# RG-LRU gates as two 64-row products side by side in the TensorE array, in two PSUM banks

## The chip, the cores and the metric

The kernel runs on one core of one Trainium2 chip. The metric is the device time of one execution in microseconds (us). Before the change the median of 3 runs is 1001.49 us (998.43 to 1003.96). TensorE multiplies a stationary operand (loaded by LDWEIGHTS) with a moving operand and writes to PSUM, of which this kernel uses banks as tiles of 128x512 fp32. VectorE (DVE), ScalarE (ACT) and GpSimd (POOL) work beside it; SyncE (SP) and POOL issue DMAs.

## The reference

One step of a decoder layer on 1024 prompt tokens and 8 decode tokens. One input projection (1024 to 7176 columns) feeds an RG-LRU branch and an mLSTM branch; both are merged and projected back. The part that the change touches is the pair of gates of the RG-LRU branch: the 1024 channels are 16 blocks of 64, and each block has its own 64x64 weights for r and for i.

```python
blocks = xc.reshape(B, S, NB_A, BW_A)            # NB_A = 16 blocks of BW_A = 64
r = sigmoid(einsum('bsnc,ncd->bsnd', blocks, w_r).reshape(B, S, W_A) + b_r)
i = sigmoid(einsum('bsnc,ncd->bsnd', blocks, w_i).reshape(B, S, W_A) + b_i)
log_a = -LRU_C * r * softplus(-lam)
a = exp(log_a)
u = sqrt(-expm1(2.0 * log_a)) * (i * xc)         # h_t = a_t h_{t-1} + u_t
```

`xc` is the branch's input after a causal convolution of width 4. The 8 decode tokens go through the same gates with their own states.

## The kernel before

Channels lie on partitions, tokens along the free dimension. Products in full precision are made from three products of float32r halves: `split` (L70 on ScalarE, L71 on VectorE) gives a high and a low part, and `mm3` (L64 to L66) multiplies high by high, high by low and low by high into one bank.

The program has an opening (normalisation, first unit), then 13 more units of the input projection, two groups of 256 columns each, every unit cut into seven products of two halves (a Strassen scheme), then the mLSTM chunks with the output projection between them. The units run from about 85 us to 660 us. `pop_bg` hands out other work between the halves of the products: gate tables, the RG-LRU queue `rgq`, the decode queue. Instructions are queued per engine, each engine works through its queue in order, and a scheduler sets the final order of each queue, so a gate's products can stand between two products of a unit.

The RG-LRU branch is worked off in 16 halves: 8 groups `j` of 128 channels (two blocks of 64) by 2 halves of 512 tokens. A half has seven steps (`rg_half`): two of convolution, `gate_r`, `gate_i`, `decay`, `scan`, `outs`. For a group the raw gate weights are put in a 128x(2x128) tile `graw`, the two blocks of r on the diagonal of one 128x128 square, those of i on that of the other; the rest was set to zero once (L639). `ghi` and `glo` are its split. A gate is then one full 128-row `mm3` into the one bank of the tag "s", read by one ScalarE tanh (L729 for r, L735 for i). Since there is one "s" bank, the products of i wait for ScalarE's reading of r. After the second half of a group, `rg_dec` does the gates of the decode tokens the same way in plain fp32, two matmuls of 8 columns (L772), each shown as two passes, with tanh in L774.

The bank of the tag "tr" serves the decode tokens of the input projection: `dec_unit` (L229, 8 matmuls with 32 stationary columns, in four groups of columns of the array) writes it once per unit, ScalarE copies it out (L232), four transposes write it again (L237), and VectorE reduces that (L240).

Of the kernel before, what the change touches and what calls it, by code (L numbers as in the profile page):

```python
# [9 lines left out]
F32 = mybir.dt.float32  # L10
F32R = mybir.dt.float32r
BF16 = mybir.dt.bfloat16
AF = mybir.ActivationFunctionType
ALU = mybir.AluOpType
# [3 lines left out]
P = 128  # L18
T = 1024
HT = 512  # L20
NB = 8
# [8 lines left out]
R_CW, R_CB, R_BR, R_BI, R_LAM, R_GM, R_H0, R_CONV, R_N0, R_END = 0, 4, 5, 6, 7, 8, 9, 17, 41, 49  # L30
# [19 lines left out]
def hymba_kernel(  # L50
# [7 lines left out]
    V, A, G, TE = nc.vector, nc.scalar, nc.gpsimd, nc.tensor  # L58
    ld = nc.sync.dma_start
    stq = nc.gpsimd.dma_start  # L60

    def mm3(out, ah, al, bh, bl, first, last):

        TE.matmul(out, ah, bh, start=first, stop=False, skip_group_check=True)  # L64
        TE.matmul(out, ah, bl, start=False, stop=False, skip_group_check=True)  # L65
        TE.matmul(out, al, bh, start=False, stop=last, skip_group_check=True)  # L66
# [12 lines left out]
    def ps(tag, shape):  # L79
        return psp.tile(shape, F32, tag=tag, name=f"ps_{tag}", bufs=NBUF.get(tag, 1))  # L80

    def const(shape, name, dt=F32):
        return cpool.tile(shape, dt, tag=name, name=name)
# [14 lines left out]
    def sg(shape, name, dt=F32):  # L98

        return stg.tile(shape, dt, tag="stg", name=name)  # L100
# [4 lines left out]
    def dconst(shape, name):  # L105

        return dpool.tile(shape, F32, tag=name, name=name)
# [10 lines left out]
    PT = dconst([P, KC, R_END], "PT")  # L118
# [5 lines left out]
    hb = const([P, KC, 2], "hb")  # L124
# [12 lines left out]
    dgr = dconst([P, 2, KC, NB], "dgr")  # L137
# [219 lines left out]
    fp = es_f.enter_context(tc.tile_pool(name="f_start", bufs=1))  # L357
# [159 lines left out]
    fp = es_f.enter_context(tc.tile_pool(name="f_gates", bufs=1, reuse_waits="tile"))  # L517

    def gates():
# [24 lines left out]
        fx, ab, lg, z, z2, p = (gx[:, n, :] for n in range(6))  # L544
# [7 lines left out]
        lfd = lg[:, 32:64].rearrange("p (b h) -> p b h", h=NH)  # L552
        V.tensor_scalar(sp2, lg[:, 64:72], -2.0, None, op0=ALU.mult)
        V.tensor_scalar(sp4n, lg[:, 64:72], 4.0, None, op0=ALU.mult)
        V.tensor_scalar(hb, PT[:, :, R_BR:R_BR + 2], 0.5, None, op0=ALU.mult)
        V.tensor_scalar(gm4, PT[:, :, R_GM], 0.25, None, op0=ALU.mult)

        dgm = fp.tile([P, 2, NB, NH], F32, tag="dgm", name="dgm")
# [48 lines left out]
        for half in range(2):  # L607
            pk = ps(("s", "qp")[half], [P, 4, P])
            for q in range(4):
                c = half * 4 + q  # L610
                TE.transpose(pk[:, q, :], stk[:, c * P:(c + 1) * P], idF)
            s = slice(half * 4, half * 4 + 4)
# [17 lines left out]
    fpr = {}  # L630

    def rd_open():

        es_f.close()
        fpr["es"] = ExitStack()
        fpr["p"] = fpr["es"].enter_context(tc.tile_pool(name="f_rd", bufs=1, reuse_waits="tile"))
        fpr["graw"] = [fpr["p"].tile([P, 2, P], F32, tag=f"graw{i}", name=f"graw{i}") for i in range(2)]
        for t in fpr["graw"]:
            G.memset(t, 0.0)  # L639
        rg_gw(0)  # L640
        stq(s_conv[0, :, 0:2, :], st_conv[0, :, 1:3, :])
        dec_open()
# [4 lines left out]
    def rg_load(n, both=False):  # L647

        if n >= len(halves) or halves[n][0] not in rst["stored"]:
            return  # L650
        j, b = halves[n]
        if ("x", n) not in rst:
            xs = fpr["p"].tile([P, 3 + HT], F32, tag="xs", name="xs", bufs=2)
            if b == 0:
                V.memset(xs[:, 0:3], 0.0)
                ld(xs[:, 3:3 + HT], d_x[j][:, 0:HT])
            else:
                ld(xs, d_x[j][:, HT - 3:T])
            rst["x", n] = xs
        if both and ("z", n) not in rst:  # L660
            rst["z", n] = zs = fpr["p"].tile([P, HT], F32, tag="zsr", name="zsr", bufs=2)
            ld(zs, d_y[j][:, b * HT:(b + 1) * HT])
# [17 lines left out]
    def rg_gw(j):  # L680
        if j < KC:
            graw = fpr["graw"][j % 2]
            for n, src in enumerate((w_rgate, w_igate)):
                for two in range(2):
                    s = slice(two * 64, two * 64 + 64)
                    ld(graw[s, n, s], src[0, 2 * j + two])

    def rg_half(j, b):
        fp = fpr["p"]
        pc = lambda r, n=1: PT[:, j, r:r + n]  # L690
        st = {}

        n = 2 * j + b

        def conv1():
            rg_load(n, True)
            xs = st["xs"] = rst["x", n]
            rg_load(n + 1)
            if b == 0:
                rg_gw(j + 1)  # L700
                ghi = fp.tile([P, 2, P], F32R, tag="ghi", name="ghi")
                glo = fp.tile([P, 2, P], F32R, tag="glo", name="glo")
                split(ghi, glo, fpr["graw"][j % 2])
                rst["g", j] = ghi, glo
            st["xc"] = xc = fp.tile([P, HT], F32, tag="xc", name="xc")
            V.tensor_scalar(xc, xs[:, 3:3 + HT], pc(R_CW + 3), pc(R_CB), op0=ALU.mult, op1=ALU.add)
            for t in (2, 1):
                V.scalar_tensor_tensor(xc, xs[:, t:t + HT], pc(R_CW + t), xc, op0=ALU.mult, op1=ALU.add)

        def conv2():  # L710
            xs, xc = st["xs"], st["xc"]
            V.scalar_tensor_tensor(xc, xs[:, 0:HT], pc(R_CW), xc, op0=ALU.mult, op1=ALU.add)
            st["xh"] = fp.tile([P, HT], F32R, tag="xh", name="xh")
            st["xl"] = fp.tile([P, HT], F32R, tag="xl", name="xl")
            split(st["xh"], st["xl"], xc)
            if b == 1:
                V.tensor_copy(OC[:, j, 1:4], xs[:, HT:HT + 3])

        def gate(g):
            ghi, glo = rst["g", j]  # L720
            pg = ps("s", [P, 512])
            mm3(pg, ghi[:, g, :], glo[:, g, :], st["xh"], st["xl"], True, True)
            return pg

        def gate_r():
            rg_load(n + 1, True)
            pg = gate(0)
            st["rg"] = fp.tile([P, HT], F32, tag="rg", name="rg")
            A.activation(st["rg"], pg, AF.Tanh, scale=0.5, bias=hb[:, j, 0:1])  # L729

        def gate_i():
            pg = gate(1)

            st["na"], st["ig"] = (fp.tile([P, HT], F32, tag=t, name=m) for m, t in (("na", "xh"), ("ig", "xl")))
            A.activation(st["ig"], pg, AF.Tanh, scale=0.5, bias=hb[:, j, 1:2])  # L735
            A.activation(st["na"], st["rg"], AF.Tanh, scale=sp2[:, j:j + 1], bias=sp2[:, j:j + 1])
            A.activation(st["rg"], st["rg"], AF.Exp, scale=sp4n[:, j:j + 1], bias=sp4n[:, j:j + 1])
            V.scalar_tensor_tensor(st["ig"], st["ig"], 1.0, st["xc"], op0=ALU.add, op1=ALU.mult)

        def decay():  # L740
            rg, na = st["rg"], st["na"]
            V.scalar_tensor_tensor(na, rg, 1.0, na, op0=ALU.add, op1=ALU.mult)
            V.tensor_scalar(rg, na, -1.0, 1.0, op0=ALU.mult, op1=ALU.add)
            V.scalar_tensor_tensor(na, na, 2.0, na, op0=ALU.subtract, op1=ALU.mult)
            A.activation(na, na, AF.Sqrt, scale=-0.25)

        def scan():
            rg, ig, na = st["rg"], st["ig"], st["na"]
            V.tensor_tensor(ig, ig, na, op=ALU.mult)
            V.tensor_tensor_scan(na, rg, ig, 0.0 if b == 0 else OC[:, j, 0:1], op0=ALU.mult, op1=ALU.add)  # L750
            V.tensor_copy(OC[:, j, 0:1], na[:, HT - 1:HT])

        def outs():
            na, zs = st["na"], rst["z", n]
            V.scalar_tensor_tensor(na, na, 0.5, zs, op0=ALU.mult, op1=ALU.mult)
            mh, ml = sg([P, HT], "rmh", F32R), sg([P, HT], "rml", F32R)
            split(mh, ml, na)
            stq(d_rm[0, j, :, b * HT:(b + 1) * HT], mh.bitcast(F32))
            stq(d_rm[1, j, :, b * HT:(b + 1) * HT], ml.bitcast(F32))
        return [conv1, conv2, gate_r, gate_i, decay, scan, outs]  # L760

    def rg_dec(j):

        pc = lambda r, n=1: PT[:, j, r:r + n]
        xc = dxc[:, j, :]
        cst = PT[:, j, R_CONV:R_CONV + 24].rearrange("p (b t) -> p b t", t=3)
        V.tensor_scalar(xc, dxz[:, 0, j, :], pc(R_CW + 3), pc(R_CB), op0=ALU.mult, op1=ALU.add)
        for t in range(3):
            V.scalar_tensor_tensor(xc, cst[:, :, t], pc(R_CW + t), xc, op0=ALU.mult, op1=ALU.add)
        pg = ps("s", [P, 2, NB])  # L770
        for g in range(2):
            TE.matmul(pg[:, g, :], fpr["graw"][j % 2][:, g, :], xc, start=g == 0, stop=True, skip_group_check=True)  # L772
        for g in range(2):
            A.activation(dgr[:, g, j, :], pg[:, g, :], AF.Tanh, scale=0.5, bias=hb[:, j, g:g + 1])  # L774

    def rg_final():

# [609 lines left out]
    for n in range(4, N):  # L1387
        c, h = n // 4, n % 4
# [83 lines left out]
```

## Time and profile before

| What | Value |
|---|---|
| runs | 998.43, 1001.49, 1003.96 us |
| profiled execution | 1000.53 us, its span 998.8 us, mean granted clock 0.993 |
| TensorE busy | 959.2 us (96% of the span), 5756 matmul passes |
| VectorE, ScalarE, GpSimd busy | 704.7, 531.7, 149.7 us |
| gate products (L64 to L66 into ps_s from xh, xl) | 96, between 147.5 and 539.9 us |
| ScalarE reads of gates (L729, L735) | 32 of 687 ns |

TensorE is pipelined: the time of a matmul in a row runs until its end in PSUM and overlaps the next one. How fast they follow one another is read from the starts.

### The profile page before, as it was taken

What the parts mean: (1) busy time and instruction counts of PE and PEld (TensorE: products, weight loads), DVE (VectorE), ACT (ScalarE), POOL (GpSimd) and SP (SyncE); (2) the same over time, 40 slices, a digit from 0 to 9 for tenths busy, and PEclk for the clock granted to TensorE, in tenths of its full rate; (3) what the DMA queues carried; (4) which work ended last, traced back from release to release, by engine and by line L of the source; (5) the groups of instructions that cost most, each with busy time, mean ns of one, the idle gap of its engine ahead of it and who ended that gap; (6) DMA issues with size and microseconds to landing.
All of it is one profiled execution on the core that took longest, in us unless ns stands there. A gap on an engine that the chain in (4) does not pass through costs nothing. (4 is left out here: it accounts for less than half of the span.)

```text
span 998.8 us, 16047 instructions
## 1 busy us (share of the span) xinstructions
PE 959.2 (96%) x5756; PEld 792.2 (79%) x5756; DVE 704.7 (71%) x1478; ACT 531.7 (53%) x950; POOL 149.7 (15%) x259
## 2 busy tenths in 40 slices
PE   8999999999999999999999999999989989899996
PEld 7887767777787988777798999987668778778776
DVE  5776798988888878767877557676556746656754
ACT  5563436675765665635667544545345535535532
POOL 1111112121212122212213110102001000000111
PEclk9999999999999999999999999999999999999999
DMA  4441357356545647266536362337746245255431
GB/s 147 143 129 42 127 141 247 129 182 202 199 152 190 189 162 225 82 217 228 193 106 212 99 195 91 117 126 250 225 141 187 86 139 165 82 155 177 107 76 55
DMA packets 125465, 152.72 MB, mean 153 GB/s; under 512 B 14119, under 2 KB 104263, under 8 KB 125376
## 3 DMA queue, kind: packets, MB, share of 16 engines
q1 hardware_dynamic: 107656, 95.81, 32.4%
q0 software_dynamic: 17728, 55.87, 15.8%
q8 instruction: 45, 0.74, 0.3%
q14 instruction: 36, 0.29, 0.1%
HBM read 100.07 MB, written 51.65 MB: 152 GB/s over the span
## 5 line engine op out<-in xcount | busy, mean ns | idle before, releaser
L71 DVE TENSOR_TENSOR wl<-raw,wh 128x1024 fp32r<-128x1024 f32 x91 | 110.9, 1219 | 32.8 <-ACT wh L70 20.4
L70 ACT CAST wh<-raw 128x1024 fp32r<-128x1024 f32 x91 | 95.4, 1049 | 69.8 <-PE ps_o L65 21.8
L64 PE MATMUL ps_kv<-cb_hi,wh 128*128 128x512 f32 x256 | 102.5, 401 | 0.4 <-ACT s L310 0.4
L65 PE MATMUL ps_kv<-cb_lo,wh 128*128 128x512 f32 x256 | 100.2, 392 | 0.0
L66 PE MATMUL ps_kv<-cb_hi,wl 128*128 128x512 f32 x256 | 100.2, 391 | 0.0
L64 PE MATMUL ps_kv<-wh,cb_hi 128*128 128x256 f32 x320 | 91.9, 287 | 0.0
L66 PE MATMUL ps_kv<-wh,cb_lo 128*128 128x256 f32 x320 | 90.7, 283 | 0.0
L65 PE MATMUL ps_kv<-wl,cb_hi 128*128 128x256 f32 x320 | 90.7, 283 | 0.0
L64 PE MATMUL ps_o<-cb_hi,wh 128*128 128x512 f32 x192 | 75.6, 394 | 0.1
L66 PE MATMUL ps_o<-cb_hi,wl 128*128 128x512 f32 x192 | 74.9, 390 | 0.0
L65 PE MATMUL ps_o<-cb_lo,wh 128*128 128x512 f32 x192 | 74.9, 390 | 0.0
L64 PE MATMUL ps_o<-wh,cb_hi 128*128 128x256 f32 x240 | 68.8, 287 | 0.0
L66 PE MATMUL ps_o<-wh,cb_lo 128*128 128x256 f32 x240 | 68.0, 283 | 0.0
L65 PE MATMUL ps_o<-wl,cb_hi 128*128 128x256 f32 x240 | 68.0, 283 | 0.0
L64 PEld LDWEIGHTS ps_kv<-wh,cb_hi 128*128 128x128 f32 x320 | 61.2, 191 | 6.5 <-issue 3.4
L64 PEld LDWEIGHTS ps_kv<-cb_hi,wh 128*128 128x128 f32 x256 | 48.1, 188 | 19.5 <-issue 5.1
L1034 DVE SCALAR_TENSOR_TENSOR W<-W,be_t,maskT 128x128 f32<-128x128 f32 x32 | 11.2, 351 | 73.6 <-DMA W<-d_alpha 73.6
L66 PEld LDWEIGHTS ps_kv<-wh,cb_lo 128*128 128x128 f32 x320 | 61.3, 191 | 1.7 <-issue 1.7
L65 PEld LDWEIGHTS ps_kv<-wl,cb_hi 128*128 128x128 f32 x320 | 61.3, 192 | 1.0 <-issue 0.8
L66 PEld LDWEIGHTS ps_kv<-cb_hi,wl 128*128 128x128 f32 x256 | 48.0, 188 | 10.4
L65 PEld LDWEIGHTS ps_kv<-cb_lo,wh 128*128 128x128 f32 x256 | 48.1, 188 | 9.4
L64 PE MATMUL ps_o<-wo,mh 128*128 128x512 f32 (+1 forms) x136 | 53.6, 394 | 0.7 <-ACT mh L70 0.7
(465 smaller groups left out, 2651.0 us busy)
## 6 DMA issues: line engine op xcount, KB each, us to landing
raw<-in_w_in_dram SPq DMA_DIRECT2D x56, 512.0 KB
Cb<-in_state_mlstm_C_dram SPq DMA_DIRECT2D x32, 256.0 KB
out_dram<-Cb POOLq DMA_DIRECT2D x32, 256.0 KB, 4.5
qk<-d_qk SPq DMA_DIRECT2D x32, 256.0 KB
oraw<-in_w_out_dram SPq DMA_DIRECT2D x16, 512.0 KB
d_qk<-s POOLq DMA_DIRECT2D x24, 256.0 KB, 4.5
x<-in_x_prompt_dram SPq DMA_DIRECT2D x8, 512.0 KB
d_x<-s POOLq DMA_DIRECT2D x16, 256.0 KB, 2.7
```

Of the source, the lines that this page charges most:

```text
L64: TE.matmul(out, ah, bh, start=first, stop=False, skip_group_check=True)
L65: TE.matmul(out, ah, bl, start=False, stop=False, skip_group_check=True)
L66: TE.matmul(out, al, bh, start=False, stop=last, skip_group_check=True)
L70: A.copy(hi, src)
L71: V.tensor_tensor(lo, src, hi.bitcast(F32), op=ALU.subtract)
L1034: V.scalar_tensor_tensor(W, W, be_t[:, c, h:h + 1], maskT, op0=ALU.add, op1=ALU.min)
```

## The change

Each half now takes both gates in one step, `gate`. The two blocks of a group lie in rows 0 to 63 and 64 to 127 of the array. `graw` is 128x128: in rows 0 to 63 the r weights of the first block stand in columns 0 to 63 and its i weights in columns 64 to 127; in rows 64 to 127 the second block's i weights stand first, and its r weights in columns 64 to 127. So one 64-row product gives r and i of a block. Products of the lower rows go to the "s" bank, products of the upper rows to the "tr" bank, in turn: three pairs, six matmuls of 64 rows by 128 columns with 512 moving columns, where there were six of 128 by 128. There are no zero quarters left, and the two memsets are gone.

The reading is now four activations on 64 partitions: r from rows 0 to 63 of "s" and rows 64 to 127 of "tr", and i from the other half of each, written to the partitions of its channels (`gate_out`). The bias table `hb` has its i column swapped to fit, by three small VectorE operations in place of one. The two ScalarE functions of r and the first VectorE operation on i move to a step `gate2`, so that a half has seven steps as before. `rg_dec` does the same with two 64-row fp32 matmuls of 8 columns, one in each bank, and four activations of 64x8.

```diff
-        fpr["graw"] = [fpr["p"].tile([P, 2, P], F32, tag=f"graw{i}", name=f"graw{i}") for i in range(2)]
-        for t in fpr["graw"]:
-            G.memset(t, 0.0)
+        fpr["graw"] = [fpr["p"].tile([P, P], F32, tag=f"graw{i}", name=f"graw{i}") for i in range(2)]
...
-                    s = slice(two * 64, two * 64 + 64)
-                    ld(graw[s, n, s], src[0, 2 * j + two])
+                    c = (n + two) % 2 * 64
+                    ld(graw[two * 64:two * 64 + 64, c:c + 64], src[0, 2 * j + two])
+    LOHI = slice(0, 64), slice(64, 128)
+    def gate_out(rg, ig, pg, j):
+        for n in range(2):
+            A.activation(rg[LOHI[n]], pg[n][LOHI[n]], AF.Tanh, scale=0.5, bias=hb[LOHI[n], j, 0:1])
+        for n in range(2):
+            A.activation(ig[LOHI[n]], pg[n][LOHI[1 - n]], AF.Tanh, scale=0.5, bias=hb[LOHI[1 - n], j, 1:2])
...
-                ghi = fp.tile([P, 2, P], F32R, tag="ghi", name="ghi")
-                glo = fp.tile([P, 2, P], F32R, tag="glo", name="glo")
+                ghi = fp.tile([P, P], F32R, tag="ghi", name="ghi")
+                glo = fp.tile([P, P], F32R, tag="glo", name="glo")
...
-        def gate(g):
+        def gate():
+            rg_load(n + 1, True)
             ghi, glo = rst["g", j]
-            pg = ps("s", [P, 512])
-            mm3(pg, ghi[:, g, :], glo[:, g, :], st["xh"], st["xl"], True, True)
-            return pg
-        def gate_r():
-            rg_load(n + 1, True)
-            pg = gate(0)
+            pg = [ps(tag, [P, 512]) for tag in ("s", "tr")]
+            for k, (w, x) in enumerate(((ghi, st["xh"]), (ghi, st["xl"]), (glo, st["xh"]))):
+                for s, o in zip(LOHI, pg):
+                    TE.matmul(o, w[s, :], x[s, :], start=k == 0, stop=k == 2)
             st["rg"] = fp.tile([P, HT], F32, tag="rg", name="rg")
-            A.activation(st["rg"], pg, AF.Tanh, scale=0.5, bias=hb[:, j, 0:1])
-        def gate_i():
-            pg = gate(1)
             st["na"], st["ig"] = ...
-            A.activation(st["ig"], pg, AF.Tanh, scale=0.5, bias=hb[:, j, 1:2])
+            gate_out(st["rg"], st["ig"], pg, j)
+        def gate2():
             A.activation(st["na"], st["rg"], AF.Tanh, ...)
...
-        return [conv1, conv2, gate_r, gate_i, decay, scan, outs]
+        return [conv1, conv2, gate, gate2, decay, scan, outs]
...
-        pg = ps("s", [P, 2, NB])
-        for g in range(2):
-            TE.matmul(pg[:, g, :], fpr["graw"][j % 2][:, g, :], xc, start=g == 0, stop=True, skip_group_check=True)
-        for g in range(2):
-            A.activation(dgr[:, g, j, :], pg[:, g, :], AF.Tanh, scale=0.5, bias=hb[:, j, g:g + 1])
+        pg = [ps(tag, [P, NB]) for tag in ("s", "tr")]
+        for s, o in zip(LOHI, pg):
+            TE.matmul(o, fpr["graw"][j % 2][s, :], xc[s, :], start=True, stop=True)
+        gate_out(dgr[:, 0, j, :], dgr[:, 1, j, :], pg, j)
```

The order of the instructions moves with it. In the rows below the names are tiles: `wh`, `wl` the halves of a unit's weights, `cb_hi`, `cb_lo` the normalised input, `ps_s`, `ps_tr`, `ps_kv`, `ps_o` the PSUM tags; the last figure is the size of the output. Line numbers after L554 are higher in the changed kernel: the gate's products are L736, the decode gates' L779, the activations L694 (r) and L696 (i).

TensorE at the first half of the first group, before: the end of the r gate and, five products later, the i gate.

```order
L65 MATMUL ps_kv<-cb_lo_167,wh_3_1556 128x512
L66 MATMUL ps_kv<-cb_hi_166,wl_3_1557 128x512
L65 MATMUL ps_s<-xl,ghi 128x512
L66 MATMUL ps_s<-xh,glo 128x512
L64 MATMUL ps_kv<-cb_hi_166,wh_3_1556 128x512
L65 MATMUL ps_kv<-cb_lo_167,wh_3_1556 128x512
L66 MATMUL ps_kv<-cb_hi_166,wl_3_1557 128x512
L64 MATMUL ps_kv<-cb_hi_166,wh_3_1556 128x512
L65 MATMUL ps_kv<-cb_lo_167,wh_3_1556 128x512
L64 MATMUL ps_s<-xh,ghi 128x512
L65 MATMUL ps_s<-xl,ghi 128x512
L66 MATMUL ps_s<-xh,glo 128x512
```

The same place after the change, with both gates:

```order
L64 MATMUL ps_o<-cb_hi_164,wh_2_1485 128x512
L736 MATMUL ps_s<-xh,ghi 128x512
L736 MATMUL ps_tr<-xh,ghi 128x512
L65 MATMUL ps_o<-cb_lo_165,wh_2_1485 128x512
L66 MATMUL ps_o<-cb_hi_164,wl_2_1486 128x512
L64 MATMUL ps_kv<-cb_hi_166,wh_3_1556 128x512
L736 MATMUL ps_s<-xl,ghi 128x512
L736 MATMUL ps_tr<-xl,ghi 128x512
L736 MATMUL ps_s<-xh,glo 128x512
L736 MATMUL ps_tr<-xh,glo 128x512
L65 MATMUL ps_kv<-cb_lo_167,wh_3_1556 128x512
```

The pairs stand next to each other everywhere. In 5 of the 16 halves full-array products of the unit come between the first pair and the other two, as here; in the other 11 the six stand in one run. That makes 21 stretches of 64-row products.

TensorE at the first decode gate, before, and after. The product of the upper rows waits for VectorE's reading of the transposes (L237) in "tr", and the scheduler has put eight products of the unit before it.

```order
L237 MATMUL ps_tr<-idF,Z 128x128 x4
L772 MATMUL ps_s<-dxc,graw_1342 128x8 x2
L64 MATMUL ps_kv<-cb_hi_160,wh_0_1745 128x512
L65 MATMUL ps_kv<-cb_lo_161,wh_0_1745 128x512
L66 MATMUL ps_kv<-cb_hi_160,wl_0_1746 128x512
```

```order
L237 MATMUL ps_tr<-idF,Z 128x128 x4
L779 MATMUL ps_s<-dxc,graw_1344 128x8
L64 MATMUL ps_kv<-cb_hi_160,wh_0_1747 128x512
L65 MATMUL ps_kv<-cb_lo_161,wh_0_1747 128x512
L66 MATMUL ps_kv<-cb_hi_160,wl_0_1748 128x512
L64 MATMUL ps_kv<-cb_hi_160,wh_0_1747 128x512
L65 MATMUL ps_kv<-cb_lo_161,wh_0_1747 128x512
L66 MATMUL ps_kv<-cb_hi_160,wl_0_1748 128x512
L64 MATMUL ps_kv<-cb_hi_160,wh_0_1747 128x512
L65 MATMUL ps_kv<-cb_lo_161,wh_0_1747 128x512
L779 MATMUL ps_tr<-dxc,graw_1344 128x8
L66 MATMUL ps_kv<-cb_hi_160,wl_0_1748 128x512
```

So it is at 4 of the 8 decode gates; at the other 4 the two stand together. That makes 12 more stretches of 64-row products.

ScalarE at the first half of the fourth group, before: the cast of the next weights (L70) and a copy of a product (L307) stand between the two gates.

```order
L307 COPY s_2819<-ps_o 128x512
L729 ACTIVATE rg<-ps_s,hb 128x512
L70 CAST wh_5_2864<-raw_5_2514 128x1024
L307 COPY s_2842<-ps_o 128x512
L735 ACTIVATE ig<-ps_s,hb 128x512
L736 ACTIVATE na<-rg,sp_93 128x512
L737 ACTIVATE rg<-rg,sp4n 128x512
L310 COPY s_2880<-ps_kv 128x512
```

After the change the four reads stand in one run, and the copy and the cast come behind them.

```order
L307 COPY s_2840<-ps_o 128x512
L694 ACTIVATE rg<-ps_s,hb 64x512
L694 ACTIVATE rg<-ps_tr,hb 64x512
L696 ACTIVATE ig<-ps_s,hb 64x512
L696 ACTIVATE ig<-ps_tr,hb 64x512
L743 ACTIVATE na<-rg,sp_93 128x512
L307 COPY s_2872<-ps_o 128x512
L744 ACTIVATE rg<-rg,sp4n 128x512
L70 CAST wh_5_2887<-raw_5_2530 128x1024
L310 COPY s_2903<-ps_kv 128x512
```

In 8 of the 14 units the next writer of "tr" after a half's gates is `dec_unit`, 17 to 73 products later; at two places it is 17.

More of the change, by code (lines that the diff above doesn't have):

```diff
@@ L554, in gates @@
         V.tensor_scalar(sp4n, lg[:, 64:72], 4.0, None, op0=ALU.mult)
-        V.tensor_scalar(hb, PT[:, :, R_BR:R_BR + 2], 0.5, None, op0=ALU.mult)
+        V.tensor_scalar(hb[:, :, 0], PT[:, :, R_BR], 0.5, None, op0=ALU.mult)
+        for s, d in ((slice(0, 64), slice(64, 128)), (slice(64, 128), slice(0, 64))):
+            V.tensor_scalar(hb[d, :, 1], PT[s, :, R_BI], 0.5, None, op0=ALU.mult)
         V.tensor_scalar(gm4, PT[:, :, R_GM], 0.25, None, op0=ALU.mult)
```

## The prediction

> **What bounds the kernel now.** I read the busy times first, then the stretch of the gates alone (from the first to the last group), then who waited for whom in it, and last the starts of single matmuls.
>
> ```profile
> PE 959.2 (96%) x5756; PEld 792.2 (79%) x5756; DVE 704.7 (71%) x1478; ACT 531.7 (53%) x950; POOL 149.7 (15%) x259
> 147.00:555.00 408.00, 404.41 (x2282) 325.90 (x2281) 325.26 (x529) 254.53 (x359) 82.78 (x137) 1.00 0.55 182
> PE ps_s L64 <- ACT rg L729: 1.9, 2, 1.7
> PE ps_s L65 <- DVE xl L71: 0.9, 1, 0.9
> PE ps_kv L64 <- ACT s L310: 0.4, 1, 0.4
> PE ps_s L64 <- ACT xh L70: 0.4, 1, 0.4
> ```
>
> In the 408 us that hold all gates TensorE is busy for 404.4 at full clock, ScalarE for 254.5, and all of TensorE's named waits come to 3.6 us. So TensorE's queue sets the pace there: what a change adds to it or takes from it is added to or taken from the total, nearly one to one. Another engine counts only where TensorE comes to wait for it.
>
> **What the gates cost now.** The starts around an i gate:
>
> ```profile
> 152.30 0.50 PE L64 MATMUL ps_s<-xh,ghi 128*128 128x512 f32 x1 [1.69 <-ACT rg L729]
> 152.63 0.39 PE L65 MATMUL ps_s<-xl,ghi 128*128 128x512 f32 x1
> 152.63 0.19 PEld L66 LDWEIGHTS ps_s<-xh,glo 128*128 128x128 f32 x1
> 152.86 0.40 PE L66 MATMUL ps_s<-xh,glo 128*128 128x512 f32 x1
> 153.10 0.39 PE L66 MATMUL ps_kv<-cb_hi,wl 128*128 128x512 f32 x1
> L64 PE MATMUL ps_s<-xh,ghi 128*128 128x512 f32 x32 | 13.3, 415 | 2.3 <-ACT rg L729 1.9 <-ACT xh L70 0.4
> ```
>
> A row lasts 0.39 us, but the next starts 0.23 us after it: 0.23 is the price. The weights of a product load while the one before runs (the PEld row starts with the L65 row). There are 3x32 = 96 gate products: 96 x 0.23 = 22.1 us. The 1.9 us is the i gate waiting for the reading of r in the single bank.
>
> **Removed.** If the two products of a pair run at once, a pair costs one slot: 48 x 0.23 = 11.0 us are gone. No row of before has two products in different rows of the array. The nearest is the decode work of a unit, four groups of 32 columns:
>
> ```profile
> L229 PE MATMUL ps_tr<-raw,hnd 128*32 128x512 f32 x224 | 28.9, 602 | 0.0
> 220.96 0.39 PE L66 MATMUL ps_kv<-cb_hi,wl 128*128 128x512 f32 x1
> 221.28 1.92 PE L229 MATMUL ps_tr<-raw,hnd 128*32 128x512 f32 x16
> 222.16 1.04 PE L229 MATMUL ps_tr<-raw,hnd 128*32 128x512 f32 x8
> 223.13 0.50 PE L64 MATMUL ps_kv<-cb_hi,wh 128*128 128x512 f32 x1
> 223.47 0.40 PE L65 MATMUL ps_kv<-cb_lo,wh 128*128 128x512 f32 x1
> ```
>
> 16 passes of 602 ns take 1.92 us, and 224 x 0.602 = 135 us of them fit in 28.9 busy us: four run at a time. I take it that two groups of rows with two banks do as much; the other bound is that they run one by one, and nothing is gained. The 1.9 us wait goes too, since i no longer waits for r; below nothing it cannot go by much, because the first pair's waits on xh and xl stay.
>
> [...]
>
> **Added: entering and leaving a tiling.** The rows above price one visit. 221.28 - 220.96 - 0.23 = 0.09 us is lost on entry. The 16 passes are four rounds; two take 222.16 - 221.28 = 0.88, so the last two should end at 223.04, and the next product starts at 223.13: 0.09 lost. Its successor comes 0.34 later, not 0.23: 0.11, the load of 128 columns of weights that nothing covers. A visit by few rows, the 49-row transposes, looks alike:
>
> ```profile
> 105.24 0.39 PE L65 MATMUL ps_kv<-cb_lo,wh 128*128 128x512 f32 x1
> 105.56 0.70 PE L539 MATMUL ps_s<-idF,par 49*128 49x49 f32 x8
> 106.19 0.51 PE L66 MATMUL ps_kv<-cb_hi,wl 128*128 128x512 f32 x1
> 106.53 0.39 PE L64 MATMUL ps_kv<-cb_hi,wh 128*128 128x512 f32 x1
> ```
>
> Entry 105.56 - 105.24 - 0.23 = 0.09; the return again 0.34 - 0.23 = 0.11. The gates' first weights have 128 columns too, so on entry another 0.11 is open. A visit then costs 0.09 + 0.11 + 0.09 + 0.11 = 0.40 us. Bounds: 0.31 if the first load on entry is hidden, 0.51 if the two halves' loads follow each other. By the order of the changed kernel there are 21 such stretches in the gates and 12 in the decode gates: 33 x 0.40 = 13.2 us (10.2 to 16.8). That is more than the pairs save.
>
> [...]
>
> **The decode gates.**
>
> ```profile
> 227.15 0.51 PE L772 MATMUL ps_s<-dxc,graw 128*128 128x8 f32 x4
> 227.52 0.48 PE L64 MATMUL ps_kv<-cb_hi,wh 128*128 128x512 f32 x1
> 227.84 0.39 PE L65 MATMUL ps_kv<-cb_lo,wh 128*128 128x512 f32 x1
> ```
>
> Four passes in 0.37 us, and the next product's successor is 0.09 late, which the price of a visit now holds: 8 x 0.09 = 0.7 us to take off. The passes stay 32 of about 0.1 us. At the 4 places where the two stand together they may overlap: 4 x 0.2 = 0.8 us at most; I take half, 0.4.
>
> **ScalarE.** What an activation costs hangs on its columns, not its partitions:
>
> ```profile
> L1200 ACT ACTIVATE fsq<-y x14: 613/626/632, 749.5 to 975.3; 128x512 bf16<-128x512 f32 x14
> L1200 ACT ACTIVATE fsq<-yd x2: 617/624/630, 971.3 to 972.4; 8x512 bf16<-8x512 f32 x2
> L735 ACT ACTIVATE ig<-ps_s,hb 128x512 f32<-128x512 f32 x16 | 11.0, 687 | 1.1 <-PE ps_s L66 0.4
> L774 ACT ACTIVATE dgr<-ps_s,hb 128x8 f32<-128x8 f32 x16 | 3.5, 264 | 0.7 <-PE ps_s L772 0.5
> L729 ACT ACT_TABLE_LOAD x5 | 6.4, 1283 | 0.1
> L70 ACT CAST wh<-raw 128x1024 fp32r<-128x1024 f32 x91 | 95.4, 1049 | 69.8 <-PE ps_o L65 21.8 <-PE ps_kv L65 19.2 <-DVE raw L255 16.8
> ```
>
> 8 partitions take as long as 128. So 32 more gate reads add 32 x 0.69 = 22.0 us and 16 more decode reads 4.2. ScalarE has 408 - 254.5 = 153 us idle in the stretch, much of it the cast of weights waiting for TensorE to free a buffer (69.8 us over the run). That idle time is the cover, and most of it holds. It fails where TensorE needs a bank soon: four reads take 2.75 us in a run, and L229 needs "tr" again. At two places only 17 products stand between, 17 x 0.23 = 3.9 us, and ScalarE may have a table load (1.28) and a cast (1.05) ahead of the reads: 5.1 us, so 1.2 us late, twice: 2.4 us. Queued behind the waiting L229 is all of TensorE. Bounds: nothing, to 6 us if the six other places (25 to 73 products) each lose 0.6 as well.
>
> **At nothing.** The memsets (POOL is idle 85%), the two more operations on `hb` and the smaller split of the weights (VectorE has 83 us idle in the stretch) lie beside TensorE. The gate weights' DMAs are as many and as large; the move of three operations into `gate2` keeps seven steps, and those operations are read by nothing on TensorE.
>
> **Sum**, on the profiled execution's 1000.53 us (0.96 under the median of the runs): -11.0 (pairs) -1.9 (wait for r) -0.7 -0.4 (decode) +13.2 (visits) +2.4 (ScalarE) = +1.6, so 1002.1 us. Its own range: low ends -11.0 - 1.9 - 0.7 - 0.8 + 10.2 = -4.2, or 996.3; high ends -11.0 - 1.9 - 0.7 + 16.8 + 6 = +9.2, or 1009.7.
>
> **The rivals.**
>
> *The pairs don't overlap.* Then 11.0 + 0.4 us come back: 1013.5 us. It decides wherever starts in a pair are 0.23 apart. For it: no row shows products in two groups of rows. Against it: four groups of columns run together.
>
> *ScalarE becomes the bound of the gates.* Two further reads make a step 1.38 us longer; if half of the 16 halves pass that on to TensorE, in the waits of L229 for "tr" or of the products that follow a late copy (L310), that is 8 x 1.38 = 11.0 in place of 2.4: 1010.7 us. It decides once ScalarE's queue behind a gate is longer than the 3.9 to 5.7 us of products that stand at most of these places. For it: the copy stands behind two more reads in the changed order. Against it: ScalarE is 62% busy there, 69% with 26 us more.
>
> *The visits cost less.* If a visit costs 0.31, decode pairs overlap and ScalarE hides, it is 996.3; if weights are also loaded ahead of entry and return (no 0.11 at all, 0.18 a visit, 5.9 us), -11.0 - 1.9 - 0.8 + 5.9 = -7.8, or 992.7, faster. Against it: both returns above show the 0.11.
>
> **How the numbers follow.** Forecast 0.58, no overlap 0.13, ScalarE 0.15, cheap visits 0.14. The likeliest gives 1002.1. A measurement of this kernel tells about 0.5%, 5 us, from no change: faster is below 996.5, slower above 1006.5. Faster: nearly all of cheap visits, 0.13. Slower: no overlap, ScalarE and little of the forecast's upper end, 0.29. Same: 0.58. The range 996 to 1011 leaves out no overlap and the cheapest visits, about 0.2.
>
> **What would show it.** Right: L736 pairs that start within about 0.01 us of each other, pair after pair 0.23 apart; first gate products 0.3 us after the last full-array product, and 0.34 between the first two products behind; no wait of ps_s on rg. ScalarE's busy time 26 us up, span of the stretch within 5 us of 408. Wrong: starts in a pair 0.23 apart; waits of L229 or ps_kv on ig of more than 3 us in sum; visits far from 0.40 us.

## The result, and the profile after

The changed kernel takes 1010.37 us (median of 4 runs, 1008.37 to 1015.59), the kernel before 1000.38 beside it: a ratio of 1.0106, with a 95% interval of 1.0065 to 1.0146. It is about 10 us slower. The forecast was 1002.1, the range 996 to 1011. The time lies in the range, but the likeliest case, no difference, did not come; "slower" had 0.29. Medians below are over all executions, while ratios and differences of means leave out the three slow ones, which took over 1.5% longer than the fastest of the same kernel.

The profiled execution took 1012.19 us with a span of 1010.4. First the busy times, then the same stretch of the gates as before (from 147 to 555 us; PE, PEld, DVE, ACT, POOL, then the granted clock).

```profile
PE 963.3 (95%) x5756; PEld 783.8 (78%) x5756; DVE 706.6 (70%) x1480; ACT 559.2 (55%) x998; POOL 148.7 (15%) x257
147.00:555.00 408.00, 400.24 (x2241) 312.17 (x2240) 324.50 (x524) 277.49 (x396) 81.90 (x135) 1.00 0.55 181
```

ScalarE has 277.5 - 254.5 = 23 us more to do in the stretch, and 27.5 more over the span, as forecast. TensorE is still busy for 400 of 408 us, but gets fewer rows done (2241 against 2282). Next, the starts around the gates of one half.

```profile
470.85 0.39 PE L66 MATMUL ps_o<-cb_hi,wl 128*128 128x512 f32 x1
471.17 0.50 PE L736 MATMUL ps_s<-xh,ghi 64*128 64x512 f32 x1
471.17 0.50 PE L736 MATMUL ps_tr<-xh,ghi 64*128 64x512 f32 x1
471.50 0.39 PE L736 MATMUL ps_s<-xl,ghi 64*128 64x512 f32 x1
471.51 0.39 PE L736 MATMUL ps_tr<-xl,ghi 64*128 64x512 f32 x1
471.74 0.39 PE L736 MATMUL ps_s<-xh,glo 64*128 64x512 f32 x1
471.74 0.39 PE L736 MATMUL ps_tr<-xh,glo 64*128 64x512 f32 x1
472.06 0.50 PE L64 MATMUL ps_o<-cb_hi,wh 128*128 128x512 f32 x1
472.39 0.39 PE L65 MATMUL ps_o<-cb_lo,wh 128*128 128x512 f32 x1
```

The two products of a pair start within 0.01 us of each other. From the row at 470.85 to the one at 472.39 there are 1.54 us: five slots of 0.23 (one ahead, three pairs, one behind) are 1.15, and the rest, 0.39, is the price of the visit. Both were forecast so. The waits of TensorE between 140 and 565 us were not (us in total, times, longest):

```profile
PE ps_s L736 <- ACT xh L70: 4.3, 4, 1.9
PE ps_tr L779 <- DVE dqk L240: 1.1, 1, 1.1
PE ps_tr L229 <- ACT ig L696: 0.7, 3, 0.3
PE ps_tr L237 <- ACT Z L232: 0.6, 1, 0.6
PE ps_tr L779 <- PE ps_s L779: 0.6, 1, 0.6
PE ps_tr L779 <- DVE do L240: 0.3, 1, 0.3
PE ps_s L736 <- DVE xl L71: 0.2, 1, 0.2
```

Before, the waits around the gates came to 3.2 us, all for rg, xl and xh. The wait for rg is gone, but the first pair now waits 4.3 us for xh, the cast that ScalarE makes. All waits with `ps_tr` in them, 3.3 us, are new: the gates have become a user of the bank of the decode work.

Where the time went along the program is seen from two groups that are the same in both kernels. The decode products of the input projection (L229) stand from the opening to the last unit, and their first and last start hold the whole stage of the gates. ScalarE's `t` (L1110, now L1116) is there once for each of 28 heads of the mLSTM chunks, and its first and last start hold that stage. Before (the last times are those of the first and last start):

```profile
L229 PE MATMUL ps_tr<-raw,hnd x224: 592/592/1062, 35.0 to 643.6; 128*32 128x512 f32 x112
L1110 ACT ACTIVATE t<-ps_qp,gi_t x28: 465/470/483, 716.6 to 969.6; 128x257 f32<-128x257 f32 x28
```

After:

```profile
L229 PE MATMUL ps_tr<-raw,hnd x224: 592/592/1062, 34.5 to 649.6; 128*32 128x512 f32 x112
L1116 ACT ACTIVATE t<-ps_qp,gi_t x28: 467/468/482, 722.7 to 981.7; 128x257 f32<-128x257 f32 x28
```

The stage of the gates became 615.1 - 608.6 = 6.5 us longer. The mLSTM stage became 259.0 - 253.0 = 6.0 us longer, although from its start on every queue holds the same instructions in the same order in both kernels, and no gate is left. The sum had no term for that stage. So there were two questions: what the gates cost where they stand, and why a stage without gates is slower.

### The profile page after: what moved, and what is told of

It reads as the page before. It is cut to its first block, busy times and chain, and to the rows that moved or that the text cites. A ratio compares the mean times of both kernels' runs of the same rounds, so it can differ in the third digit from the quotient of the medians.

```text
span 1010.4 us, 16123 instructions
## 1 busy us (share of the span) xinstructions
PE 963.3 (95%) x5756; PEld 783.8 (78%) x5756; DVE 706.6 (70%) x1480; ACT 559.2 (55%) x998; POOL 148.7 (15%) x257
## 5 line engine op out<-in xcount | busy, mean ns | idle before, releaser
L70 ACT CAST wh<-raw 128x1024 fp32r<-128x1024 f32 x91 | 95.3, 1048 | 68.0 <-PE ps_kv L65 21.2
```

The costliest lines, as they stand in the source:

```text
L70: A.copy(hi, src)
```

## The experiments

Each kernel ran beside the kernel before on the same chip. A 2x2 came first: products in 128 or 64 rows, two or four reads; all of these take both gates in one step with two banks.

**The changed kernel again.** No edit.

> The changed kernel once more, beside the experiments of the same call. The profile before it puts 5.3 us of the loss ahead of the last unit (the product stage, up to about 555 us) and 6.7 us behind it, where the order of TensorE is the same in both kernels. Theory 'late loss by chance': the loss in the product stage comes back at 4 to 6 us, the loss behind it does not (0 +- 3 us), and the total is about 1006. Theory 'late loss belongs to the change': both come back, total 1010.

Measured: 1010.81 us (999.04 to 1016.17, 10 runs), ratio 1.010 (1.0058 to 1.0143). The loss is real and as large as before. Its profiled execution:

```profile
L229 PE MATMUL ps_tr<-raw,hnd x224: 592/592/1062, 32.2 to 644.1; 128*32 128x512 f32 x112
L1116 ACT ACTIVATE t<-ps_qp,gi_t x28: 467/470/482, 717.7 to 977.7; 128x257 f32<-128x257 f32 x28
```

Here the gates' stage is 611.9 us, 3.3 more than before, and the mLSTM stage 260.0, 7.0 more. (The stage starts 2.8 us earlier than before because the opening was that much shorter in this execution, so this profile as a whole lies 7.6 us above the one of before.) So both losses come back; their sizes differ by a few us from one execution to another.

**Both gates in one step, with full products and two reads.** This is the kernel before with only the step and the banks of the change; the decode gates stay as they were. (In the diff the two old steps are shortened to notes.)

```diff
-        def gate_r(): ...      (one mm3 into "s", one read)
-        def gate_i(): ...      (one mm3 into "s", one read)
+        def gate():
+            pg = [ps(tag, [P, 512]) for tag in ("s", "tr")]
+            for g in range(2):
+                mm3(pg[g], ghi[:, g, :], glo[:, g, :], st["xh"], st["xl"], True, True)
+            for g, dst in enumerate((st["rg"], st["ig"])):
+                A.activation(dst, pg[g], AF.Tanh, scale=0.5, bias=hb[:, j, g:g + 1])
```

> Products of 128 rows as before, but both gates in one step in the two banks s and tr, read by two activations of 128 partitions. No 64-row products, no further reads. Theory 'visits to the 64-row tiling and their waits': the wait of i for r (1.9 us) is gone and nothing is added, 997 to 1001 us, and no loss in the product stage. Theory 'two banks, or the one step, cost it' (tr shared with the decode products, late copies of ScalarE): 1004 to 1010 us.

Measured: 991.71 us (989.28 to 993.65, 5 runs), ratio 0.9911 (0.9879 to 0.9943). It beats both kernels, and both theories on record (997 to 1001, 1004 to 1010). The one step and the second bank were not tried apart. Of TensorE's waits between 140 and 565 us one is left:

```profile
PE ps_s L64 <- ACT xh L70: 1.6, 1, 1.6
```

and its two stages:

```profile
L229 PE MATMUL ps_tr<-raw,hnd x224: 592/592/1062, 34.9 to 641.2; 128*32 128x512 f32 x112
L1105 ACT ACTIVATE t<-ps_qp,gi_t x28: 466/469/483, 713.9 to 962.9; 128x257 f32<-128x257 f32 x28
```

The gates' stage gains 2.3 us, about the wait for r. The mLSTM stage gains 4.0 us more, with its order unchanged. The same stage that loses in the changed kernel gains here.

**The same with four reads.** Each bank is read by two activations of 64 partitions.

```diff
-                A.activation(dst, pg[g], ...)
+                for h in (slice(0, 64), slice(64, 128)):
+                    A.activation(dst[h], pg[g][h], ...)
```

> As e2, but each bank read by two activations of 64 partitions, so ScalarE has the 22 us of further gate reads of the change and no 64-row product. Theory 'ScalarE': 1006 to 1011 us, most of the loss. Theory 'visits': within 2 us of e2.

Measured: 1003.36 us (1000.76 to 1010.01, 10 runs), ratio 1.0034 (1.0005 to 1.0064). Two further reads a half cost 11.6 us, so the theory that they are nearly free ("visits") falls, though the total stays below what "ScalarE" gave, 1006 to 1011. The stages of the profiled execution (1010.01 us, at the upper end of its runs):

```profile
L229 PE MATMUL ps_tr<-raw,hnd x224: 592/592/1062, 34.8 to 642.4; 128*32 128x512 f32 x112
L1106 ACT ACTIVATE t<-ps_qp,gi_t x28: 465/468/482, 714.8 to 979.5; 128x257 f32<-128x257 f32 x28
```

Against two reads the gates' stage is 1.3 us longer (607.6 against 606.3), the mLSTM stage 15.7 us. Together that is 17 us in this pair of executions, where the medians differ by 11.6.

**Products in 64 rows, two reads.** The changed kernel, but each bank of the prompt is read by one activation of 128 partitions. This leaves out the exchange of r and i in the second block of each group, so r and i of that block are mixed up.

```diff
-            gate_out(st["rg"], st["ig"], pg, j)
+            for g, dst in enumerate((st["rg"], st["ig"])):
+                A.activation(dst, pg[g], AF.Tanh, scale=0.5, bias=hb[:, j, g:g + 1])
```

> The changed kernel with each bank of the prompt gates read by one activation of 128 partitions: r and i of the second block change places, so that part of the computation is left out; the decode gates keep four reads. 64-row products and visits stay, 22 us of ScalarE go. Theory 'ScalarE': falls to 1000 to 1002 us. Theory 'visits and the waits of the gates for their operands': within 2 us of the changed kernel (1007 to 1011).

Measured: 1001.23 us (994.61 to 1005.44, 10 runs), ratio 1.0012 (0.9983 to 1.0041). Waits and stages:

```profile
PE ps_s L736 <- ACT xh L70: 3.0, 3, 1.4
PE ps_tr L780 <- PE ps_kv L66: 0.3, 1, 0.3
PE ps_s L736 <- DVE xl L71: 0.2, 1, 0.2
```

```profile
L229 PE MATMUL ps_tr<-raw,hnd x224: 592/592/1062, 32.2 to 637.1; 128*32 128x512 f32 x112
L1117 ACT ACTIVATE t<-ps_qp,gi_t x28: 462/468/482, 711.4 to 969.2; 128x257 f32<-128x257 f32 x28
```

With two reads fewer, nearly all waits with `ps_tr` are gone. The gates' stage takes 604.9 us, 3.7 less than before and 7.0 less than in the changed kernel's second profile: in the stage where they stand, the products in 64 rows are no loss with two reads. Four reads cost 7.0 us there with these products and 1.3 with the full ones, so it is the two together that lose. By the totals the reads cost 9.6 us with these products and 11.6 with the full ones; the products in 64 rows (prompt and decode) cost 9.5 us with two reads and 7.5 with four. Of these four sums the gates' stage shows 7.0, 1.3, -1.4 and 4.3, so the reads with these products cost mainly in that stage, while the reads with full products, and the products with two reads, cost nearly all behind it. The mLSTM stage is 257.8 us here, 4.8 more than before.

**What stalls in the mLSTM stage.** TensorE stalls there, in most chunks once or twice, before the product of vh and ph. Around the longest such stall of the changed kernel, from three engines (SP's row is the issue of a load):

```profile
922.30 4.66 SPq L1025 DMA_DIRECT2D so<-d_so  x1
932.36 0.32 SPq L1015 DMA_DIRECT2D W<-d_alpha  x1
935.55 0.35 DVE L1040 SCALAR_TENSOR_TENSOR W<-W,be_t,maskT 128x128 f32<-128x128 f32 x1 [2.56 <-DMA W<-d_alpha]
935.94 0.31 ACT L1041 ACTIVATE W<-W 128x128 f32<-128x128 f32 x1 [3.27 <-DVE W L1040]
936.97 0.47 ACT L1116 ACTIVATE t<-ps_qp,gi_t 128x257 f32<-128x257 f32 x1
937.49 0.38 PE L64 MATMUL ps_qp<-vh,ph 128*128 128x258 f32 x1 [3.27 <-ACT t L1116]
```

Read upward: the product needs the bank that `t` reads, `t` stands behind the exponential of W in ScalarE's queue, W waits for VectorE, VectorE for the load, and the load stood in SP's queue behind others, of which `so` held the queue for 4.66 us. Such a chain would make a late engine issue late loads, so that the next chunk is late again; that it does so is argued from the order, and the next experiments were to test it. The waits of that product between 660 us and the end of the stage, before and after:

```profile
PE ps_qp L64 <- ACT t L1110: 11.9, 8, 2.8
```

```profile
PE ps_qp L64 <- ACT t L1116: 14.4, 9, 3.3
```

**Other loads in the mLSTM stage.** To see whether the difference of the kernels belongs to the gates or to that chain, W got a third buffer in four kernels (pf overwrites W to make room).

```diff
-        W = mx["p"].tile([P, L], F32, tag="W", name="W", bufs=2)
+        W = mx["p"].tile([P, L], F32, tag="W", name="W", bufs=3)    (loaded by w_load)
...
-        pf = mx["p"].tile([P, L], F32, tag="pf", name="pf")
+        pf = d["W"]
...
+        w_load(n + 2)
         m_a(n)
```

> The kernel before, with the mLSTM stage's load of the decay row (tile W) issued one head earlier: a third buffer for W, found by letting pf overwrite W. The gates are those of before. Theory 'loop' (the late loss comes from a chain in the mLSTM stage: a late load on SP's queue, a late W, a stall of TensorE once a chunk, a half-clock window after it): the stall of 1.3 to 3.0 us before the product of vh and ph shrinks below 0.8 us in every chunk, fewer half-clock windows, total 990 to 996. Rival 'direct' (that stall is set by something else than W's load): 998 to 1002, stalls as before.

> The changed kernel with the same earlier load of W. Theory 'loop': what is left against the kernel before with the earlier W is the loss in the product stage alone, +3 to +5 us (994 to 1000). Rival 'direct' (the gates of 64 rows cost the late stage something of their own): +9 to +11 us against it, as without the earlier W.

> Products of 128 rows for both gates in one step and two banks, two reads, with the earlier W. Theory 'loop': -3 us against the kernel before with the earlier W (987 to 993): what the one step gains in the product stage by the marks. Rival 'direct': -8 us, as without the earlier W.

> The same with each bank read by two activations of 64 partitions (four reads), with the earlier W. Theory 'loop': +1 to +3 us against two reads (988 to 996), the part of the 11.7 us that the product stage showed. Rival 'direct': +9 to +12 us against two reads: the reads of themselves cost that much.

The edit did less than was meant: the scheduler did not issue W a head earlier. W only changed places in SP's queue with loads beside it, from chunk to chunk in the same way in all four kernels. Measured, the edited ones with 10 runs each beside a kernel before of 1000.64 us:

| gates | loads as they were | edited loads of W |
|---|---|---|
| before | 1000.2 | 997.32, ratio 0.9953 (0.9922 to 0.9984) |
| changed | 1010.8 | 998.68, ratio 0.9983 (0.9949 to 1.0017) |
| full, two reads | 991.7 | 996.57, ratio 0.9967 (0.9931 to 1.0003) |
| full, four reads | 1003.4 | 995.47, ratio 0.9938 (0.9907 to 0.9969) |

From a spread of 19 us the four come within 3.2. The change costs 1.4 us in place of 10, and the two further reads -1.1 in place of +11.6; by the means of the runs 1.2 ± 3.3 and -1.7 ± 3.3. "Direct" falls: neither the gates nor the reads cost the mLSTM stage a fixed amount. "Loop" fits the sizes of the differences, but not the stall, which did not shrink in the kernel before (13.8 us of these waits after 11.9). The gain of the plain one step is gone too: 0.8 us are left of 8.5. The changed kernel with edited loads, first this wait, then its two stages:

```profile
PE ps_qp L64 <- ACT t L1124: 9.1, 11, 3.3
```

```profile
L229 PE MATMUL ps_tr<-raw,hnd x224: 592/592/1059, 35.1 to 650.2; 128*32 128x512 f32 x112
L1124 ACT ACTIVATE t<-ps_qp,gi_t x28: 466/469/482, 724.0 to 968.3; 128x257 f32<-128x257 f32 x28
```

Its gates' stage is 615.1 us, as long as without the edit, and its mLSTM stage 244.3 in place of 259.0. The profile of the kernel before with the same loads has 609.2 and 250.9. So in these two executions the loss where the gates stand remains, 5.9 us, and the mLSTM stage gains 6.6: the small difference of the totals is made of two large ones, and not of the gates' loss alone, as "loop" had it.

**Two queues.** Beside the edit of W, so and z are loaded from POOL's queue.

```diff
-            ld(sos[n], d_so[h][c * L:(c + 1) * L, :])
+            (ld if c == 0 else stq)(sos[n], d_so[h][c * L:(c + 1) * L, :])
...
-                ld(z[:, h, :], d_zs[h][c * L:(c + 1) * L, :])
+                stq(z[:, h, :], d_zs[h][c * L:(c + 1) * L, :])
```

> The kernel before with the earlier W of the former runs and, beside it, the mLSTM stage's loads of so and z issued from POOL's queue in place of SP's, so that W is no longer queued behind their waits. The gates are those of before. Theory 'loop' (the mLSTM stage loses what its chain of loads makes it lose, and the gates only set how it is entered): stalls before the product of vh and ph under 0.8 us in nearly every chunk, total 985 to 993. Rival (the stall comes from elsewhere): 995 to 1000, stalls of 1 to 3.5 us as with the earlier W alone.

> The changed kernel with the same two edits of the loads. Theory 'loop': against the kernel before with these edits only the loss of the product stage is left, +3 to +5.5 us. Rival 'direct' (the change costs the late stage something whatever its loads do): +9 us or more. Rival 'nothing' (with an even late stage the change is free): within 1.5 us.

> Products of 128 rows, both gates in one step and two banks, two reads, with the same two edits of the loads. Theory 'loop': -2 to -4 us against the kernel before with these edits, what the product stage showed (475.1 against 478.3 us between the same two products). Rival 'direct': -8 us, as without the edits. Expected to be the fastest: 982 to 990.

Measured: 1010.57 us (998.52 to 1015.32, 8 runs), ratio 1.0076 (1.0034 to 1.0118), with the gates of before; 1008.52 (998.49 to 1012.13, 12 runs), ratio 1.0072 (1.0043 to 1.0102), with the changed ones; 1000.56 (994.89 to 1009.73, 12 runs), ratio 1.0007 (0.9975 to 1.0039), with full products in one step. The repair failed: all three are slower than with the edit of W alone. The chain did not go, since W is still queued behind the loads of vt and qk; and so now waits in POOL's queue. Of the waits of POOL in the kernel with the gates of before:

```profile
POOL so L1027 <- ACT so L1143: 97.2, 14, 12.1
```

With these loads the change is not slower than the gates of before (-2.1 us; -0.1 ± 4.7 by the means), and the full products are 10.0 us faster (6.3 ± 4.8). "Direct" falls for the change once more (it had +9). The forecasts of "loop", +3 to +5.5 for the change and -2 to -4 for the full products, are not borne out by the medians, but the intervals of the means reach into them.

**A mere delay.** Last, the kernel before was only made to come later to that stage: the i gate of the last half is computed seven times, and all queues behind it keep their order.

```diff
         def gate_i():
+            if n == 15:
+                for _ in range(6):
+                    gate(1)
             pg = gate(1)
```

> The kernel before, with the i gate of the last of the 16 halves computed seven times in place of once: 18 more products of 0.233 us at about 540 us, 4.2 us of TensorE in all, and the same result. All that follows stands in the same order as before. Theory 'entry' (the mLSTM stage loses or gains several us by when and in what state it is entered): the total differs from before by something else than +4.2, by at least 3 us (below +1 or above +7.2). Rival 'constant' (that stage takes the same time however late it is entered): +3 to +5.5 us.

Measured: 1007.8 us (1001.64 to 1012.01, 10 runs) against 998.29, ratio 1.0097 (1.0063 to 1.0131). 4.2 us of products cost 9.5 us (9.8 ± 3.0 by the means). So "constant", +3 to +5.5 us, falls (the interval starts at 6.3), and "entry" is borne out by the totals: a delay of the size of the gates' own loss, with the gates of before, gives a loss as large as that of the change. The profiled execution, the second fastest of the ten at 1005.26 us, shows the delay but not what is added to it:

```profile
L229 PE MATMUL ps_tr<-raw,hnd x224: 592/592/1059, 35.0 to 648.8; 128*32 128x512 f32 x112
L1113 ACT ACTIVATE t<-ps_qp,gi_t x28: 466/470/483, 722.3 to 974.3; 128x257 f32<-128x257 f32 x28
```

613.8 us is 5.2 more than before, 252.0 a us less. So where the slower executions of this kernel lose the rest isn't seen in a trace.

## Why the prediction was right and wrong

For the gates' stage the gaps between TensorE's starts were summed, between two products of the input projection that are the same in both kernels (at 77 and 556 us before): 478.3 us before, 483.4 and 481.3 in two executions of the changed kernel, so +5.1 and +3.0, where the sum said +1.6 for the whole. (The L229 rows reach over a longer stretch.) The gaps that touch a gate product, less 0.233 us for each product of the unit among them, give the gates alone; likewise for the decode gates. By its steps, for the first of the two executions:

| step of the prediction | forecast us | measured us |
|---|---|---|
| pairs, and 21 visits (measured up to the first product behind) | -11.0 + 8.4 = -2.6 | 23.4 to 18.0: -5.4 |
| the wait for r goes | -1.9 | waits 3.2 to 4.5: +1.3 |
| decode gates, and 12 visits | -1.1 + 4.8 = +3.7 | 3.4 to 7.7: +4.3, of it 2.0 waits |
| ScalarE's reads, at L229 | +2.4 | +1.1 at L229, +1.2 at the other small products, L237 among them |
| nothing | 0 | +2.8 between products of the unit, about 2 of it the end of the visits |
| sum | +1.6 | +5.3 (the window says +5.1) |

- **Pairs overlap: right.** Every gate pair starts together. The rival that they don't is out.
- **A visit costs 0.40 us: right.** The first row of the table stops at the first product behind a visit. The second one is late too: the median gap ahead of it is 0.335 us, where the same gap was 0.231 before, and for 21 visits that makes the 2 us among the products of the unit. Taken whole, from the product ahead to the second one behind, less their slots and any wait, 16 of the 21 visits of the second execution cost 0.38 to 0.48 us, four beside products of 256 columns 0.39, and one 0.72. That is 8.7 us, where the sum had 8.4.
- **The wait for r goes: the step that failed first.** It went, but "the first pair's waits on xh and xl stay" was wrong as a price: xh was waited for 0.4 us in all, and is now for 4.3, at 4 places. With two reads the wait is 3.0 (64 rows) and 1.6 (full products), so part of it goes with ScalarE's reads; what makes the rest was not looked for.
- **ScalarE: right mechanism, mis-sized and misplaced.** L229 was late by 0.2 to 0.3 us at three places, not by 1.2 at two. But the reads' bank is also that of the decode gates and of the transposes: 2.0 us of waits at L779 and 0.6 at L237, which the sum did not hold. The experiment with two reads takes nearly all of it away. The rival "ScalarE becomes the bound" has the right time (1010.7) and the right culprit, but not its mechanism: of its 11 us through waits of L229 and late copies, the table has 2.3.
- **The number: inside the range by luck.** The upper part of the range was made of visits at 0.51 us and of six more late L229, and neither came. The loss came from waits for xh, from the decode gates and from a stage that the sum left out.
- **The end of the program: not in the sum at all.** "What a change adds to it or takes from it is added to or taken from the total, nearly one to one" holds in the gates' stage and failed behind it. In the profiled executions 6 to 7 of the 10 us arise in the mLSTM stage. The prediction should have looked at who is waited for there: stalls of TensorE of up to 2.8 us, 11.9 in all, stood in the profile before.

What that stage is made of can be read in the traces. Between the first and last start of `t` TensorE's waits can be added up, and the periods in which its granted clock is at half can be counted; each lasts 3.41 us and costs up to 1.7 (last section).

| profiled execution | mLSTM stage, us | TensorE's waits in it | half-clock periods | rest |
|---|---|---|---|---|
| before | 253.0 | 17.6 | 2 | 232.0 |
| changed | 259.0 | 20.9 | 3 | 233.0 |
| changed, again | 260.0 | 18.3 | 5 | 233.2 |
| full products, two reads | 249.0 | 14.7 | 1 | 232.6 |
| full products, four reads | 264.7 | 20.3 | 8 | 230.8 |
| 64 rows, two reads | 257.8 | 17.9 | 4 | 233.1 |
| changed, edited loads of W | 244.3 | 11.5 | 1 | 231.1 |
| before, delayed | 252.0 | 16.9 | 1 | 233.4 |

The rest, at 1.7 us a period, is the same within 3 us, while the stage varies by 20. So of the 15.7 us between two and four reads up to 11.9 are seven more half-clock periods. Over all executions on record the clock's part is smaller: the span times the share of the clock that was not granted is 7.7 us in the mean of the kernel before, 9.6 in the changed kernel beside it (11.6 in the four executions of the result), and 5.7 and 10.0 with two and four reads. That is 2 to 4 us of the 9 to 11 for the change and 4 of 13 for the reads.

What stays open is why one kernel meets more of these waits and periods than another. A delay alone gives a loss in the totals (9.5 us for 4.2) and other loads reverse it, but no trace shows the path from the entry to the loss.

## What to carry to other kernels

Row tiling made two 64-row products as cheap as one (0.23 us from one pair to the next, as from one full product to the next), but each excursion of three pairs cost 0.40 us of a saving of 0.69, and packing two results into halves of two banks doubled the reads; here the plain use of a second bank, both gates in one step, was worth more (991.7 us) than the tiling, though only 0.8 us with the edited loads. Before a second bank is taken, list who else writes it. And where the end of a program runs in a chain of loads that TensorE waits for, a change of 5 us upstream came out as 10 with one order of loads and as 1 with another: measure the stage where the change stands beside the total, and run a plain delay as a control.

## What the runs showed of the hardware

The half-clock periods. The waits shown above are shorter than the time that they cost, since TensorE's clock fell to half behind some of them. In the changed kernel the very first pair waits for xh:

```profile
149.51 0.50 PE L736 MATMUL ps_s<-xh,ghi 64*128 64x512 f32 x1 [1.87 <-ACT xh L70]
```

One us later such a period begins, and there is another in the mLSTM stage (busy times of the engines, and the clock as the third column from the end):

```profile
150.60:154.00 3.40, 3.40 (x10) 1.99 (x9) 3.05 (x8) 3.35 (x6) 1.45 (x2) 0.50 0.96 297
860.60:864.00 3.40, 3.14 (x11) 2.85 (x12) 3.06 (x8) 0.62 (x2) 0.00 (x0) 0.50 0.06 18
```

Each such period lasts 3.413 us in the trace's record of the clock (or twice that, where two follow one another) and by an estimate, half of that at a clock of 0.50, costs up to 1.7 us; 0.9 us of the one at 150.6 is in the +2.8 of the table. The stretches of the same length just ahead of these two, and a third one behind which the clock stayed full:

```profile
147.19:150.60 3.41, 1.54 (x7) 0.69 (x6) 3.41 (x8) 1.41 (x3) 0.56 (x1) 1.00 0.85 270
857.20:860.61 3.41, 1.15 (x7) 0.67 (x6) 1.02 (x3) 1.30 (x4) 0.00 (x0) 0.99 0.29 72
894.70:898.11 3.41, 1.65 (x11) 1.17 (x10) 0.65 (x3) 0.41 (x2) 0.00 (x0) 1.00 0.58 152
```

TensorE was busy for 45%, 34% and 48% of them. The stretches at full clock between two such periods are whole multiples of their length: in the changed kernel 580.27 us behind the one at 150.6, 170 of them, and 34.13 us ahead of the one at 860.6, ten. So the 14 traces were divided into windows of 3.413 us in step with these periods, from 60 us on and up to 25 us before the end, and the picture is the same. In 33 windows its rows fill less than 43%, and a half-clock window follows every one; in 32 they fill 43 to 54%, and it follows 8; in 3636 more at full clock they fill more, and it follows none. So what counted here is how much of a stall falls into one window, and that can differ from one execution to the next: the changed kernel had 3 such periods in the mLSTM stage of its first profile and 5 in that of its second. A window need not be idle as a whole for that: behind the one with a wait of 1.87 us, 45% of it busy, the clock was at half. In the kernel with full products and four reads these periods recur with the chunks, by the same view:

```profile
780.20:783.60 3.40, 3.40 (x12) 2.82 (x11) 2.01 (x7) 1.13 (x4) 0.00 (x0) 0.51 0.44 128
817.80:821.20 3.40, 3.40 (x13) 2.91 (x12) 2.31 (x8) 1.13 (x4) 0.00 (x0) 0.50 0.32 93
855.30:858.70 3.40, 3.40 (x13) 3.11 (x14) 2.78 (x7) 0.41 (x1) 0.00 (x0) 0.51 0.11 33
892.90:896.30 3.40, 3.15 (x11) 2.87 (x12) 3.05 (x8) 0.60 (x2) 0.00 (x0) 0.50 0.03 9
```

They are 37.5 or 37.6 us apart, eleven such windows, and that is close to a chunk's mean length (264.7 us for 27 heads in this run, so 39.2 for the four of a chunk); the kernel with two reads has one such period in that stage. Whether the two lock to each other, and so keep the stage slow, was not tried; it is one way in which a later entry could change a stage's time.
